# VectorE's instruction order and the 16x16 inverse in the chunk pipeline of a bidirectional encoder layer

## The chip, the cores and the metric

One NeuronCore of a Trainium2 chip runs the whole program. The metric is the device time of one execution in microseconds; a measurement is the median of several executions. Engines: PE (TensorE), DVE (VectorE), ACT (ScalarE), POOL (GpSimd) and SP (SyncE, which here issues all DMAs).

## The reference

Two layers of an encoder are applied to 2,560 tokens (a sequence of 2,048 and one of 512). Layer 0 holds two gated linear recurrences. Layer 1 holds a banded attention (8 heads, window 128) and an RWKV-7 time mixing (8 heads of 64, both directions). The change touches layer 1 alone. The part of it that the kernel has to compute in chunks is the scan

```
def step(S, inp):
    r_t, w_t, k_t, v_t, kk_t, b_t = inp
    s_kk = jnp.einsum('bhvk,bhk->bhv', S, kk_t)
    S = S * w_t[:, :, None, :] - s_kk[..., None] * b_t[:, :, None, :] + v_t[..., None] * k_t[:, :, None, :]
    return S, jnp.einsum('bhvk,bhk->bhv', S, r_t)
```

In chunks of 64 tokens this needs, for each chunk and head, the inverse of a 64x64 unit triangular matrix, some Gram products, and a short sequential chain over chunks. The attention beside it is

```
s = jnp.einsum('bnigrd,bnjgd->bngrij', qb, kb).astype(jnp.float32) * (hd ** -0.5)
lse = jnp.logaddexp(jax.nn.logsumexp(s, axis=-1), sink_b)
p = jnp.exp(s - lse[..., None])
```

## The kernel before

The program runs layer 0, then layer 1's projections, then `layer1_core` (the stage of this change), then the output projection. `layer1_core` has 20 steps (4 head pairs by 5 blocks of 512 tokens; each step holds both directions, 16 chunk-heads of 128 rows). Its work is written as generators ("lanes"), each `yield` ending one round's share, and a loop over rounds takes one share of every lane in the order C, T, A, X:

- A (`stageA`, 10 rounds a step, five for each half): Gram products `gramb`, `gramk`, then `bk`, `kt`, `av`; DVE multiplies them with masks into `GB`, ACT copies, POOL sorts the 32x32 diagonal blocks into `LD` and `OF`. In the sixth round (second half) it also builds `LC` from the 16x16 blocks (`L1` on POOL, `LC` on DVE) and stores it to DRAM (`lm`). `load` prefetches the next half's `Z`, `KR`, `vs` by DMA, four buffers deep.
- `inverse` (called whole at the end of every tenth round, round 8 of each step): reads `lm` back as `A`, so that each of 128 partitions holds one 16x16 block; inverts it on DVE by back substitution, 14 times a product into `tp` and an add into `A` (L1370, L1372); stores it to DRAM (`tm`), reads it back as `TC`, and spreads it into `TE` and, transposed, `TT` (L1378, L1380).
- T (`stageT`, 10 rounds, starting at round 12 with the first step): with `TE` and `TT` it doubles the blocks to 32 and 64 rows (`px`, `py`, DVE and ACT evacuate), then for each half `t1` (ACT copies it), `finx` (DVE adds it into `RX`) and `fino` (ACT copies it into `OH`).
- C (`chain`, 8 rounds of each 10, starting at round 20): 16 small matmuls `chain`, then one DVE add that makes the next state `S0` (named S in the trace); every fourth time DVE also adds the outputs into `od`, which go to DRAM.
- X (`attention`, 40 units of five rounds): scores of two heads, scores of two more with the normalisation on DVE (`nm`, `se`, `den`, `rd`, four scalings of `pr`, with ACT's exponentials between), `po` and DVE's `yo`, and two rounds of transposes `pt`.

A scheduler orders each engine's queue from a simulated timeline, program order deciding among what is ready there. PE alone is exempt: inside this stage `pin` ties each matmul to the one before it, so PE's queue follows the source order. The queues of DVE, ACT, POOL and SP are the scheduler's. Every engine takes its own queue strictly in order, so an instruction that waits holds all behind it.

PSUM tiles: `pg` and `pT` (lanes A and T) hold one buffer each, `pa` (attention: `score`, `pt`, `po`) two, so PE can often start a lane's next product only when DVE or ACT has read the one before.

Of the kernel before, what the change touches and what calls it, by code (L numbers as in the profile page):

```python
# [10 lines left out]
F32 = mybir.dt.float32  # L11
# [4 lines left out]
ALU = mybir.AluOpType  # L16
# [22 lines left out]


class Common:
    def __init__(self, ctx, tc, a, seqs):
        self.ctx, self.tc, self.nc, self.a = ctx, tc, tc.nc, a
        self.seqs = seqs
        self.T = sum(n for _, n in seqs)
        self.nblk = self.T // NB
        self.blk_seq = []
        for s, (o, n) in enumerate(seqs):
            self.blk_seq += [s] * (n // NB)
        nc = self.nc  # L50
        self.const = ctx.enter_context(tc.tile_pool(name="const", bufs=1))
        self.dram = ctx.enter_context(tc.tile_pool(name="dram", bufs=1, space=DRAM))
        self.lanes = {}
        self.pt_tag = "t"
        self.pinned = []
        nc.scalar.preload_act_table_set("natural_log_exp_and_others")
        self.eps6 = self.cst("eps6", 1e-6)
        self.eps5 = self.cst("eps5", 1e-5)
        self.ident = self.load_const("ident", [128, 128])
        self.ones = self.const.tile([128, 128], F32R, name="onesm")  # L60
        self.act(self.ones, self.ident, AF.Copy, bias=1.0 / 128.0, scale=0.0)
# [53 lines left out]
    def tt(self, out, a, b, op, eng=None):  # L115
        (eng or self.nc.vector).tensor_tensor(out=out, in0=a, in1=b, op=op)  # L116

    def stt(self, out, a, s, b, op0, op1, eng=None):
        (eng or self.nc.vector).scalar_tensor_tensor(out=out, in0=a, scalar=s, in1=b, op0=op0, op1=op1)  # L119

    def ts(self, out, a, s1, s2, op0, op1=None, eng=None):
        eng = eng or self.nc.vector
        if op1 is None:
            eng.tensor_scalar(out=out, in0=a, scalar1=s1, scalar2=None, op0=op0)
        else:
            eng.tensor_scalar(out=out, in0=a, scalar1=s1, scalar2=s2, op0=op0, op1=op1)

    def mm(self, out, lhsT, rhs, start=True, stop=True):
        self.pin(self.nc.tensor.matmul(out=out, lhsT=lhsT, rhs=rhs, start=start, stop=stop))  # L129

    def pin(self, ins):

        if self.pinned:
            if len(self.pinned) > 1:
                self.tc.add_manual_dep(ins.ins, self.pinned[1], mybir.DependencyInfo(
                    mybir.DependencyClass.NoSync, mybir.DependencyReason.DATA), reason="order")
            self.pinned = [True, ins.ins.name]

# [11 lines left out]
    def tr(self, out, in_):  # L150
        n = in_.shape[0]
        self.pin(self.nc.tensor.transpose(out, in_, self.ident[0:n, 0:n]))  # L152

# [693 lines left out]
class Odd(Even):  # L847
# [369 lines left out]
    def layer1_core(self):  # L1217
        tc, nc, a = self.tc, self.nc, self.a
        with ExitStack() as ctx:
# [46 lines left out]

            loaded = []

# [21 lines left out]
            def stageA(n):  # L1290
# [4 lines left out]
                LO = lp.tile([128, 16, 32], F32, tag="LO", bufs=2, name="LO")  # L1295
                data[n] = (OF, LO)
                for hf in range(2):
                    cs = slice(4 * hf, 4 * hf + 4)
# [12 lines left out]
                    for hd in range(2):  # L1311
                        for i, blk in enumerate((B1[hd], B2[hd])):
                            nc.gpsimd.tensor_copy(b4(LD)[blk, :, cs], gs[blk, :, :, 32 * i:32 * i + 32])
                    if hf == 1:

                        LC = lp.tile([128, 16, 16], F32, tag="LC", bufs=1, name="LC")
                        L1 = lp.tile([128, 16, 16], F32, tag="L1", bufs=1, name="L1")
                        self.tt(L1, LD[:, :, 16:32], M1, ALU.mult, nc.gpsimd)
                        self.tt(LC, LD[:, :, 0:16], M0, ALU.mult)
                        self.tt(LC, LC, L1, ALU.add)  # L1320
                        nc.sync.dma_start(out=lms[n % 2].rearrange("d c p t -> p (d c) t"), in_=LC)
                        nc.gpsimd.memset(LO[:, :, 0:16], 0.0)
                        self.tt(LO[:, :, 16:32], LD[:, :, 16:32], MO, ALU.mult, nc.gpsimd)
                    for hd in range(2):
# [37 lines left out]
            def inverse(n):  # L1362

                A = self.wk.tile([128, 16, 16], F32, tag="A", bufs=2, name="A")
                nc.sync.dma_start(out=A, in_=lms[n % 2].rearrange("d c (g s) t -> (d c g) s t", s=16))
                tp = self.wk.tile([128, 64], F32, tag="tp", bufs=1, name="tp")
                for j in range(14, 0, -1):
                    w = 15 - j
                    t3 = tp[:, 0:j * w].rearrange("p (a b) -> p a b", b=w)
                    self.tt(t3, A[:, 0:j, j:j + 1].to_broadcast([128, j, w]),  # L1370
                            A[:, j:j + 1, j + 1:16].to_broadcast([128, j, w]), ALU.mult)
                    self.tt(A[:, 0:j, j + 1:16], A[:, 0:j, j + 1:16], t3, ALU.add)  # L1372
                nc.vector.memset(A[:].rearrange("p a b -> p (a b)")[:, 0:256:17], 1.0)
                nc.sync.dma_start(out=tms[n % 2].rearrange("d c (g s) t -> (d c g) s t", s=16), in_=A)
                TC = lp.tile([128, 16, 16], F32, tag="TC", bufs=1, name="TC")
                nc.sync.dma_start(out=TC, in_=tms[n % 2].rearrange("d c p t -> p (d c) t"))
                te, tt = small("TE"), small("TT")
                self.tt(te.rearrange("p c (a t) -> p c a t", t=16),  # L1378
                        TC.unsqueeze(2).to_broadcast([128, 16, 2, 16]), ME, ALU.mult)
                nc.vector.transpose(out=tt, in_=te)  # L1380
                tes.append(te)
                tts.append(tt)

            def stageT(n):
# [17 lines left out]
                self.tt(te, te, y, ALU.add)  # L1402
                nc.vector.transpose(out=tt, in_=te)
                for i in range(2):
# [9 lines left out]
                nc.scalar.copy(xs[B2[0]], x[B2[0]])  # L1414
                nc.vector.tensor_copy(xs[B2[1]], x[B2[1]])
                yield
# [4 lines left out]
                nc.scalar.copy(TL[B1[0], :, 32:64], y[B1[0]])  # L1421
                nc.vector.tensor_copy(TL[B1[1], :, 32:64], y[B1[1]])
                yield
# [40 lines left out]
            def chain(n):  # L1464
# [7 lines left out]
                for hf in range(2):  # L1472
# [3 lines left out]
                    for c in range(4):  # L1476
                        if S0[0] is None:
                            S0[0] = OH[:, :, 0, 64:128]
                            for d in range(2):
                                nc.vector.tensor_copy(o4[d][:, 0], OH[:, d, 0, 0:64])  # L1480
                            i = 1
                        else:
                            z = S0[0]
                            for d in range(2):
                                for q in Q:
                                    self.mm(po[q, d, 4 + c], RX[q, d, c, 64:128], z[q, d])
                            for d in range(2):
                                for q in Q:
                                    self.mm(po[q, d, c], z[q, d], RX[q, d, c, 0:64])
                            s0 = self.wk.tile([128, 2, 64], F32, tag="S0", bufs=3, name="S0")  # L1490
                            self.tt(s0, po[:, :, 4 + c], OH[:, :, c, 64:128], ALU.add)
                            S0[0] = s0
# [19 lines left out]
            self.ln_exp()  # L1512
            self.pinned = [True]
            lanes = dict(C=seq(chain), T=seq(stageT), A=seq(stageA), X=self.attention())
            start = dict(A=0, X=0, T=12, C=20)
            for r in range(5 * (2 * N + 6)):
                for x in ("C", "T", "A", "X"):
                    if r < start[x] or x == "C" and (r - start[x]) % 5 == 4:
                        continue
                    next(lanes[x], None)  # L1520
                if r >= 8 and (r - 8) % 10 == 0 and (r - 8) // 10 < N:
                    inverse((r - 8) // 10)
                self.tick()
            assert all(next(g, "end") == "end" for g in lanes.values())
            self.pinned = []
            self.drain()
# [82 lines left out]
    def attend(self, g, b, qt, s0, s1, keys, msk, snk, nsk):  # L1609
# [17 lines left out]
        for hd in range(4):  # L1627
            ps = self.pa.tile([128, 384], F32, tag="s", name="score")
            for i in range(2):
                self.mm(ps[:, 0:nk], q[:, hd], K[:, i, k0 - w0:k1 - w0], start=(i == 0), stop=(i == 1))  # L1630
            pr = ap.tile([128, 384], F32, tag="ptmp", bufs=5, name="pr")
            h = 4 * g + hd
            nc.vector.tensor_tensor_reduce(pr[:, 0:nk], ps[:, 0:nk], msk[:, m0:m0 + nk], -0.125,  # L1633
                                           nsk[:, h:h + 1], ALU.add, ALU.min, nm[:, hd:hd + 1])
# [9 lines left out]
        rd = ap.tile([128, 4], F32, tag="rd", name="rd")  # L1644
        nc.vector.reciprocal(out=rd, in_=den)
        for hd in range(4):
# [134 lines left out]
```

## Time and profile before

| what | us |
|---|---|
| median of 3 runs (lowest, highest) | 4200.91 (4189.49, 4204.29) |
| the profiled execution, device time | 4210.02 |
| its span from first to last instruction | 4208.2 |
| PE busy over the span | 3572.8 (85%) |
| DVE busy | 2432.1 (58%) |
| ACT busy | 1900.4 (45%) |
| POOL busy | 844.1 (20%) |
| mean granted TensorE clock, share of full | 0.916 |

The profiled execution's own time is 2 us above its span and 9 us above the median of the three runs. Layer 1's core takes the span from about 2,640 to 3,870 us; its steady part repeats with one step of 10 rounds. Busy shares are averages over four stages with different limits, so the stage has to be read by itself.

### The profile page before, as it was taken

The page shows a single profiled execution, that of the slowest core. Times are in us where ns is not written, and L with a number is a line of the kernel's source. Part 1 is how long each engine was busy: PE and PEld are TensorE (multiplying, and loading weights), DVE is VectorE, ACT ScalarE, POOL GpSimd, SP SyncE. Part 2 cuts the span into 40 slices and gives each one's busy share as a digit, 9 for nine tenths or more (in the row PEclk, how much of TensorE's full clock was granted, in tenths as well). Part 3 has the DMA queues.
Part 4 walks back from the last instruction along what each step waited for, and adds up shares of the span by engine and source line. Part 5 has one row for each costly group of instructions (what it writes and reads, how often), then busy time and mean ns, then how long its engine had stood idle before and what let it go on. Part 6 is the DMA issues. An engine that isn't in the chain of part 4 may idle for free.

```text
span 4208.2 us, 95158 instructions
## 1 busy us (share of the span) xinstructions
PE 3572.8 (85%) x39928; PEld 2865.3 (68%) x39928; DVE 2432.1 (58%) x4888; ACT 1900.4 (45%) x3394; POOL 844.1 (20%) x1013
## 2 busy tenths in 40 slices
PE   6999999998888699998999898687777777776689
PEld 4878787776776578776777676466556666655477
DVE  4554545457666678466574757445445455444687
ACT  4565657455455532355463446333333333333450
POOL 1020212112222232224132322222112111211000
PEclk8999999999899799999999999788888888887799
DMA  7544544456545488677677775533333333333685
GB/s 274 200 153 153 187 149 175 167 183 235 221 180 204 136 261 268 221 248 237 239 269 229 238 260 203 145 89 99 106 94 92 100 100 84 96 99 99 200 294 186
DMA packets 646285, 754.43 MB, mean 179 GB/s; under 512 B 188352, under 2 KB 512576, under 8 KB 620256
## 3 DMA queue, kind: packets, MB, share of 16 engines
q1 hardware_dynamic: 645856, 748.34, 54.2%
q8 instruction: 314, 5.14, 0.5%
q14 instruction: 115, 0.94, 0.1%
HBM read 518.51 MB, written 220.20 MB: 176 GB/s over the span
## 4 chain that ended last, share of the span: by engine, by line
PE 27%; DMA 9%; DVE 7%; issue 5%; ACT 2%; POOL 2%; SPq 1%; DVEq 0%; POOLq 0%; ACTq 0%
PE pp L129 13%; DMA lm<-LC 2%; PE po L129 1%; PE chain L129 1%; DVE tp L116 1%; DMA h<-h_scr 1%; PE py L129 1%; PE px L129 1%; DVE A L116 1%; PE pt L152 1%; DMA A<-lm 1%; PE fino L129 1%; PE gramb L129 1%; DMA tm<-A 1%; PE score L129 1%
## 5 line engine op out<-in xcount | busy, mean ns | idle before, releaser
L129 PE MATMUL pp<-h,whi 128*128 128x512 f32 (+2 forms) x4800 | 1570.4, 406 | 100.0 <-DMA h<-h_scr 42.1
L129 PEld LDWEIGHTS pp<-h,whi 128*128 128x128 f32 (+2 forms) x4800 | 896.6, 191 | 316.0 <-DMA h<-h_scr 45.0
L129 PE MATMUL pp<-h,wlo 128*128 128x512 f32 (+2 forms) x2400 | 960.2, 401 | 6.1 <-POOL wlo L116 6.0
L129 PEld LDWEIGHTS pp<-h,wlo 128*128 128x128 f32 (+2 forms) x2400 | 456.7, 190 | 114.7 <-POOL wlo L116 9.2
L113 ACT ACT_TABLE_LOAD x227 | 291.2, 1283 | 22.9 <-DVE cl L506 12.4
L129 PE MATMUL pp<-owh,oh 128*128 128x512 f32 x640 | 255.9, 400 | 21.7 <-DMA oh<-o_scr 21.7
L129 PE MATMUL pp<-owh,ol 128*128 128x512 f32 x640 | 251.4, 394 | 4.9 <-DMA ol<-o_scr 4.9
L129 PE MATMUL pp<-owl,oh 128*128 128x512 f32 x640 | 253.6, 396 | 0.0
L116 POOL TENSOR_TENSOR wlo<-wst,whi 128x512 fp32r<-128x512 f32 (+3 forms) x87 | 158.3, 1826 | 278.4 <-ACT whi L113 267.5
L1635 ACT ACTIVATE pr<-pr,nm 128x384 f32<-128x384 f32 (+1 forms) x160 | 93.8, 587 | 240.7 <-DVE nm L1633 217.0
L116 POOL TENSOR_TENSOR tmp<-tmp 128x512 fp32r<-128x512 f32 x80 | 120.7, 1509 | 238.5 <-ACT tmp L113 175.9
L116 POOL TENSOR_TENSOR at<-abuf,abuf 64x256 f32<-64x256 f32 x80 | 63.9, 799 | 517.8 <-DVE abuf L536 448.2
L152 PE MATMUL pt<-c_ident,pr 128*128 128x128 f32 x448 | 77.3, 303 | 102.9 <-DVE yo L116 91.9
L129 PEld LDWEIGHTS pp<-owh,oh 128*128 128x128 f32 x640 | 122.7, 192 | 49.6 <-DMA oh<-o_scr 24.5
L129 PEld LDWEIGHTS pp<-owh,ol 128*128 128x128 f32 x640 | 121.5, 190 | 32.4 <-DMA ol<-o_scr 6.8
L1633 DVE CUSTOM_DVE_ANT_0 pr<-score,amask,nsink 128x384 f32<-128x384 f32 (+1 forms) x160 | 88.3, 585 | 90.6 <-PE score L129 90.5
L129 PEld LDWEIGHTS pp<-owl,oh 128*128 128x128 f32 x640 | 122.9, 192 | 25.1
L113 ACT ACTIVATE tmp<-tmp 128x512 fp32r<-128x512 f32 (+2 forms) x165 | 103.7, 629 | 67.5 <-DVE tmp L119 50.8
L152 PEld LDWEIGHTS pt<-c_ident,pr 128*128 128x128 f32 x448 | 51.6, 151 | 118.5 <-issue 103.0
L129 PE MATMUL po<-pT,vw 128*128 128x512 f32 x224 | 122.8, 687 | 5.2 <-DVE nm L1633 4.7
L129 PE MATMUL score<-kw,q 128*128 128x384 f32 (+1 forms) x320 | 86.6, 398 | 42.2 <-DVE nm L1633 30.5
L116 DVE TENSOR_TENSOR tp<-A 128x14 f32<-128x14 f32 (+6 forms) x280 | 65.2, 233 | 95.9 <-DMA A<-lm 87.8
(325 smaller groups left out, 7301.8 us busy)
## 6 DMA issues: line engine op xcount, KB each, us to landing
h<-h_scr SPq DMA_DIRECT2D x70, 2048.0 KB, 9.1
h<-h_scr SPq DMA_DIRECT2D x80, 1024.0 KB, 7.4
z_scr<-Z SPq DMA_DIRECT2D x40, 1024.0 KB, 5.0
h_scr<-h SPq DMA_DIRECT2D x10, 2048.0 KB, 7.4
oh<-o_scr SPq DMA_DIRECT2D x40, 512.0 KB, 5.0
ol<-o_scr SPq DMA_DIRECT2D x40, 512.0 KB, 6.4
h_scr<-h1s SPq DMA_DIRECT2D x20, 1024.0 KB, 4.9
Zc<-z_scr SPq DMA_DIRECT2D x80, 256.0 KB, 3.5
```

The lines of the kernel that those rows point to most:

```text
L113: self.nc.scalar.activation(out=out, in_=in_, func=func, bias=bias, scale=scale)
L116: (eng or self.nc.vector).tensor_tensor(out=out, in0=a, in1=b, op=op)
L129: self.pin(self.nc.tensor.matmul(out=out, lhsT=lhsT, rhs=rhs, start=start, stop=stop))
L152: self.pin(self.nc.tensor.transpose(out, in_, self.ident[0:n, 0:n]))
L1633: nc.vector.tensor_tensor_reduce(pr[:, 0:nk], ps[:, 0:nk], msk[:, m0:m0 + nk], -0.125, nsk[:, h:h + 1], ALU.add, ALU.min, nm[:, hd:hd + 1])
L1635: nc.scalar.activation(out=pr[:, 0:nk], in_=pr[:, 0:nk], func=AF.Exp, bias=nm[:, hd:hd + 1], scale=-1.0, accum_out=den[:, hd:hd + 1])
```

## The change

A small class `InOrder` wraps an engine: each instruction issued through it gets an ordering dependency (without a semaphore) on the one before it. Inside the round loop both `self.pe` and `self.vec` are such wrappers, and the helpers `tt`, `stt`, `ts` and the direct DVE calls of this stage go through `self.vec`; so DVE's queue now follows the source order as PE's did. (`pin` is gone; PE's order is made by the same class.)

`inverse` becomes a lane, I, last in each round and starting at round 6, with yields that spread it over 10 rounds. Counting rounds of a step from A's first, 0 to 9: round 6 builds `LC` and issues the store and the read-back; rounds 8 and 9 do five back-substitution columns each; round 0 of the next step does the last four, stores and reads back; round 2 makes `TE` and `TT`; T's first round is now round 3. `L1` moves from POOL to DVE; `LC`, `L1` and `LO` move from lane A into lane I. T and C start one round later (13 and 21 for 12 and 20).

```
+class InOrder:
+    def __init__(self, tc, eng):
+        self.tc, self.eng, self.prev = tc, eng, None
+
+    def __getattr__(self, name):
+        def call(*args, **kwargs):
+            ins = getattr(self.eng, name)(*args, **kwargs)
+            if self.prev is not None:
+                self.tc.add_manual_dep(ins.ins, self.prev, mybir.DependencyInfo(
+                    mybir.DependencyClass.NoSync, mybir.DependencyReason.DATA), reason="order")
+            self.prev = ins.ins.name
+            return ins
+        return call
...
     def tt(self, out, a, b, op, eng=None):
-        (eng or self.nc.vector).tensor_tensor(out=out, in0=a, in1=b, op=op)
+        (eng or self.vec).tensor_tensor(out=out, in0=a, in1=b, op=op)
...
     def mm(self, out, lhsT, rhs, start=True, stop=True):
-        self.pin(self.nc.tensor.matmul(out=out, lhsT=lhsT, rhs=rhs, start=start, stop=stop))
+        self.pe.matmul(out=out, lhsT=lhsT, rhs=rhs, start=start, stop=stop)
...
@@ stageA @@
-                    if hf == 1:
-
-                        LC = lp.tile([128, 16, 16], F32, tag="LC", bufs=1, name="LC")
-                        L1 = lp.tile([128, 16, 16], F32, tag="L1", bufs=1, name="L1")
-                        self.tt(L1, LD[:, :, 16:32], M1, ALU.mult, nc.gpsimd)
-                        self.tt(LC, LD[:, :, 0:16], M0, ALU.mult)
-                        self.tt(LC, LC, L1, ALU.add)
-                        nc.sync.dma_start(out=lms[n % 2].rearrange("d c p t -> p (d c) t"), in_=LC)
-                        nc.gpsimd.memset(LO[:, :, 0:16], 0.0)
-                        self.tt(LO[:, :, 16:32], LD[:, :, 16:32], MO, ALU.mult, nc.gpsimd)
@@ inverse @@
+                LD, LO = diag.pop(n)
+
+                LC = lp.tile([128, 16, 16], F32, tag="LC", bufs=1, name="LC")
+                L1 = lp.tile([128, 16, 16], F32, tag="L1", bufs=1, name="L1")
+                self.tt(L1, LD[:, :, 16:32], M1, ALU.mult)
+                self.tt(LC, LD[:, :, 0:16], M0, ALU.mult)
+                self.tt(LC, LC, L1, ALU.add)
+                nc.sync.dma_start(out=lms[n % 2].rearrange("d c p t -> p (d c) t"), in_=LC)
+                nc.gpsimd.memset(LO[:, :, 0:16], 0.0)
+                self.tt(LO[:, :, 16:32], LD[:, :, 16:32], MO, ALU.mult, nc.gpsimd)
                 A = self.wk.tile([128, 16, 16], F32, tag="A", bufs=2, name="A")
                 nc.sync.dma_start(out=A, in_=lms[n % 2].rearrange("d c (g s) t -> (d c g) s t", s=16))
+                yield
+                yield
                 tp = self.wk.tile([128, 64], F32, tag="tp", bufs=1, name="tp")
                 for j in range(14, 0, -1):
...
                     self.tt(A[:, 0:j, j + 1:16], A[:, 0:j, j + 1:16], t3, ALU.add)
-                nc.vector.memset(A[:].rearrange("p a b -> p (a b)")[:, 0:256:17], 1.0)
+                    if j in (10, 5):
+                        yield
+                self.vec.memset(A[:].rearrange("p a b -> p (a b)")[:, 0:256:17], 1.0)
                 nc.sync.dma_start(out=tms[n % 2].rearrange("d c (g s) t -> (d c g) s t", s=16), in_=A)
                 TC = lp.tile([128, 16, 16], F32, tag="TC", bufs=1, name="TC")
                 nc.sync.dma_start(out=TC, in_=tms[n % 2].rearrange("d c p t -> p (d c) t"))
+                yield
+                yield
                 te, tt = small("TE"), small("TT")
...
-                nc.vector.transpose(out=tt, in_=te)
+                self.vec.transpose(out=tt, in_=te)
                 tes.append(te)
                 tts.append(tt)
+                for _ in range(4):
+                    yield
...
@@ the round loop @@
-            self.pinned = [True]
-            lanes = dict(C=seq(chain), T=seq(stageT), A=seq(stageA), X=self.attention())
-            start = dict(A=0, X=0, T=12, C=20)
+            self.pe, self.vec = InOrder(tc, nc.tensor), InOrder(tc, nc.vector)
+            lanes = dict(C=seq(chain), T=seq(stageT), A=seq(stageA), X=self.attention(), I=seq(inverse))
+            start = dict(A=0, X=0, I=6, T=13, C=21)
             for r in range(5 * (2 * N + 6)):
-                for x in ("C", "T", "A", "X"):
-                    if r < start[x] or x == "C" and (r - start[x]) % 5 == 4:
-                        continue
-                    next(lanes[x], None)
-                if r >= 8 and (r - 8) % 10 == 0 and (r - 8) // 10 < N:
-                    inverse((r - 8) // 10)
+                for x in ("C", "T", "A", "X", "I"):
+                    if r >= start[x] and not (x == "C" and (r - start[x]) % 5 == 4):
+                        next(lanes[x], None)
                 self.tick()
```

## Rows read from the trace of the kernel before

**Rows 1.** Engine busy over 19 whole steps of the stage (span, engines, clock, DMA).
```profile
2681.90:3815.60 1133.70, 858.55 (x24792) 702.56 (x24792) 556.73 (x1678) 398.81 (x884) 211.28 (x389) 0.86 0.35 94
```

**Rows 2.** The transpose that ends the inverse, by its source line.
```profile
L1380 DVE STREAM_TRANSPOSE TT<-TE x20: 711/711/714, 2681.9 to 3815.6; 128x512 f32<-128x512 f32 x20
```

**Rows 3.** Who waited for whom, 2660 to 3800 us: total, times, longest.
```profile
PE pt L152 <- DVE yo L116: 90.7, 19, 11.0
...
DVE tp L116 <- DMA A<-lm: 87.8, 20, 5.7
...
DVE TE L116 <- DMA TC<-tm: 77.9, 19, 6.1
...
PE fino L129 <- DVE RX L116: 36.6, 13, 6.1
...
PE score L129 <- DVE nm L1633: 27.1, 7, 5.2
...
PE px L129 <- issue: 19.5, 16, 2.5
...
PE kt L129 <- issue: 17.5, 8, 3.2
...
PE bk L129 <- issue: 17.1, 9, 2.2
...
PE score L129 <- DVE A L1373: 10.8, 3, 3.7
```

**Rows 4.** Timeline of DVE within one step: start, duration, instruction, idle before.
```profile
3010.14 0.42 DVE L116 TENSOR_TENSOR LC<-LC,L 128x256 f32<-128x256 f32 x1
...
3016.30 0.17 DVE L116 TENSOR_TENSOR tp<-A 128x14 f32<-128x14 f32 x1 [3.54 <-DMA A<-lm]
...
3027.71 0.17 DVE L116 TENSOR_TENSOR A<-A,tp 128x14 f32<-128x14 f32 x1
3027.80 0.85 DVE L116 TENSOR_TENSOR yo<-po,gt 64x256 f32<-64x256 f32 x2
3032.96 0.69 DVE L116 TENSOR_TENSOR TE<-TC,mkb 128x512 f32<-128x512 f32 x1 [4.30 <-DMA TC<-tm]
3033.68 0.71 DVE L1380 STREAM_TRANSPOSE TT<-TE 128x512 f32<-128x512 f32 x1
3034.43 1.23 DVE L116 TENSOR_TENSOR RX<-finx,KR 128x1024 f32<-128x1024 f32 x1
...
3047.87 0.62 DVE L1633 CUSTOM_DVE_ANT_0 pr<-score,amask,nsink 128x384 f32<-128x384 f32 x1
...
3050.07 1.41 DVE L124 TENSOR_SCALAR pr<-pr,rd 128x384 f32<-128x384 f32 x4
```

**Rows 5.** Timeline of PE around the same step.
```profile
3002.50 1.10 PE L129 MATMUL gramb<-KR,Zc 64*64 64x128 f32 x32
...
3004.34 0.45 PE L129 MATMUL chain<-S,RX 64*64 64x64 f32 x8
...
3028.80 0.87 PE L152 MATMUL pt<-c_ident,pr 128*128 128x128 f32 x3 [5.96 <-DVE yo L116]
...
3031.87 1.93 PE L129 MATMUL gramb<-KR,Zc 64*64 64x128 f32 x32
```

**Rows 6.** Instruction groups, 2660 to 3800 us: count, busy us, mean ns, idle before.
```profile
L116 DVE TENSOR_TENSOR tp<-A 128x14 f32<-128x14 f32 (+6 forms) x267 | 62.5, 234 | 95.5 <-DMA A<-lm 87.8
...
L116 POOL TENSOR_TENSOR LO<-LD,mkb 128x256 f32<-128x256 f32 x20 | 14.6, 731 | 0.0
L116 DVE TENSOR_TENSOR LC<-LC,L 128x256 f32<-128x256 f32 x20 | 14.6, 729 | 18.5 <-POOL L L116 18.5
...
L116 DVE TENSOR_TENSOR LC<-LD,mkb 128x256 f32<-128x256 f32 x19 | 8.1, 425 | 13.9 <-POOL LD L1313 13.9
```

**Rows 7.** The prefetch of KR: one issue in SP's timeline.
```profile
3035.68 0.91 SPq L1283 DMA_DIRECT2D KR<-z_scr  x2
```

**Rows 8.** DMA issues, 2660 to 3800 us: count, KB each, median us to landing.
```profile
KR<-z_scr SPq DMA_DIRECT2D x72, 256.0 KB, 3.2
```

More of the change, by code (lines that the diff above doesn't have):

```diff
@@ L54, in __init__ @@
         self.pt_tag = "t"
-        self.pinned = []
+        self.pe, self.vec = nc.tensor, nc.vector
         nc.scalar.preload_act_table_set("natural_log_exp_and_others")
@@ L115, in tt @@
     def tt(self, out, a, b, op, eng=None):
-        (eng or self.nc.vector).tensor_tensor(out=out, in0=a, in1=b, op=op)
+        (eng or self.vec).tensor_tensor(out=out, in0=a, in1=b, op=op)
     def stt(self, out, a, s, b, op0, op1, eng=None):
-        (eng or self.nc.vector).scalar_tensor_tensor(out=out, in0=a, scalar=s, in1=b, op0=op0, op1=op1)
+        (eng or self.vec).scalar_tensor_tensor(out=out, in0=a, scalar=s, in1=b, op0=op0, op1=op1)
     def ts(self, out, a, s1, s2, op0, op1=None, eng=None):
-        eng = eng or self.nc.vector
+        eng = eng or self.vec
         if op1 is None:
@@ L128, in mm @@
     def mm(self, out, lhsT, rhs, start=True, stop=True):
-        self.pin(self.nc.tensor.matmul(out=out, lhsT=lhsT, rhs=rhs, start=start, stop=stop))
[L131 to L137, printed above, removed]
+        self.pe.matmul(out=out, lhsT=lhsT, rhs=rhs, start=start, stop=stop)
     def split(self, x, hi, lo, eng=None):
@@ L151, in tr @@
         n = in_.shape[0]
-        self.pin(self.nc.tensor.transpose(out, in_, self.ident[0:n, 0:n]))
+        self.pe.transpose(out, in_, self.ident[0:n, 0:n])
     def ln_exp(self):
@@ L1265, in layer1_core @@
             tms = [self.dram.tile([2, 8, 128, 16], F32, name=f"tm{i}") for i in range(2)]
-            loaded = []
+            loaded, diag = [], {}
             def load(u):
@@ L1296, in stageA @@
                 data[n] = (OF, LO)
+                diag[n] = (LD, LO)
                 for hf in range(2):
@@ L1402, in stageT @@
                 self.tt(te, te, y, ALU.add)
-                nc.vector.transpose(out=tt, in_=te)
+                self.vec.transpose(out=tt, in_=te)
                 for i in range(2):
@@ L1414, in stageT @@
                 nc.scalar.copy(xs[B2[0]], x[B2[0]])
-                nc.vector.tensor_copy(xs[B2[1]], x[B2[1]])
+                self.vec.tensor_copy(xs[B2[1]], x[B2[1]])
                 yield
@@ L1421, in stageT @@
                 nc.scalar.copy(TL[B1[0], :, 32:64], y[B1[0]])
-                nc.vector.tensor_copy(TL[B1[1], :, 32:64], y[B1[1]])
+                self.vec.tensor_copy(TL[B1[1], :, 32:64], y[B1[1]])
                 yield
@@ L1479, in chain @@
                             for d in range(2):
-                                nc.vector.tensor_copy(o4[d][:, 0], OH[:, d, 0, 0:64])
+                                self.vec.tensor_copy(o4[d][:, 0], OH[:, d, 0, 0:64])
                             i = 1
@@ L1512, in layer1_core @@
             self.ln_exp()
-            self.pinned = [True]
-            lanes = dict(C=seq(chain), T=seq(stageT), A=seq(stageA), X=self.attention())
-            start = dict(A=0, X=0, T=12, C=20)
+            self.pe, self.vec = InOrder(tc, nc.tensor), InOrder(tc, nc.vector)
+            lanes = dict(C=seq(chain), T=seq(stageT), A=seq(stageA), X=self.attention(), I=seq(inverse))
+            start = dict(A=0, X=0, I=6, T=13, C=21)
             for r in range(5 * (2 * N + 6)):
-                for x in ("C", "T", "A", "X"):
-                    if r < start[x] or x == "C" and (r - start[x]) % 5 == 4:
-                        continue
-                    next(lanes[x], None)
-                if r >= 8 and (r - 8) % 10 == 0 and (r - 8) // 10 < N:
-                    inverse((r - 8) // 10)
+                for x in ("C", "T", "A", "X", "I"):
+                    if r >= start[x] and not (x == "C" and (r - start[x]) % 5 == 4):
+                        next(lanes[x], None)
                 self.tick()
             assert all(next(g, "end") == "end" for g in lanes.values())
-            self.pinned = []
+            self.pe, self.vec = nc.tensor, nc.vector
             self.drain()
@@ L1632, in attend @@
             h = 4 * g + hd
-            nc.vector.tensor_tensor_reduce(pr[:, 0:nk], ps[:, 0:nk], msk[:, m0:m0 + nk], -0.125,
+            self.vec.tensor_tensor_reduce(pr[:, 0:nk], ps[:, 0:nk], msk[:, m0:m0 + nk], -0.125,
                                            nsk[:, h:h + 1], ALU.add, ALU.min, nm[:, hd:hd + 1])
@@ L1644, in attend @@
         rd = ap.tile([128, 4], F32, tag="rd", name="rd")
-        nc.vector.reciprocal(out=rd, in_=den)
+        self.vec.reciprocal(out=rd, in_=den)
         for hd in range(4):
```

## The prediction

> **What bounds the kernel now.** I read the busy time of the stage first, then the waits, then one step in the timelines of DVE and PE. The change leaves the other stages alone, so its worth is read from `layer1_core`. From the first to the twentieth transpose that ends an inverse the trace has 19 equal steps [rows 2]: (3815.6 - 2681.9)/19 = 59.67 us each. In that stretch PE is busy 858.55 us, 45.2 a step, and so idle 14.5 us a step; DVE is busy 556.73/19 = 29.3 us a step, ACT 21.0, POOL 11.1 [rows 1]. No engine is full. Since PE's queue is in source order and every lane passes through it, the stage is as long as PE's work plus PE's waits.
>
> The list of waits says what those are [rows 3]; it covers 1140 us, 19.1 steps. PE waited 90.7 us at `pt` for DVE's `yo`, 36.6 at `fino` for `RX`, 27.1 and 10.8 at `score` for DVE: 165.2 us, 8.65 a step. Another 19.5 + 17.5 + 17.1 = 54.1 us, 2.83 a step, are waits of PE at `px`, `kt` and `bk` that are put to "issue": PE waited for nothing that the profile shows. And DVE itself, idle half of the time, waited 87.8 us for `A` and 77.9 for `TC`, the two trips of the inverse through DRAM: 8.7 a step, as much as PE lost to DVE.
>
> The timeline shows how one becomes the other [rows 4, 5]. DVE adds up `LC` until 3010.56; the first use of `A` starts at 3016.30, after 3.54 us of idle DVE. The back substitution ends at 3027.88 and only then does `yo` run, although `po` had been ready long before: it stands behind the inverse in DVE's queue. PE's transposes share their two buffers with `po`, so they sat idle 5.96 us until 3028.80. Then `TE`, next in DVE's queue, waits 4.30 us for `TC`, and `RX`, which needs nothing of the inverse, runs behind it at 3034.43; `fino` needs `RX`. The scheduler placed the inverse as if its DMAs came back sooner than they do.
>
> [...] The same 32 `gramb` matmuls took 1.10 us before this wait and 1.93 us 3 us after it [rows 5].
>
> **The change, part by part.** All positions are rounds 0 to 9 of a step; a round is 4.5 us of PE work on average (45.2/10).
>
> Waits for the two trips. `LC` is now done at the end of round 6 and `A` first used at the end of round 8; the last column is done in round 0 and `TE` made at the end of round 2. Each trip has some two rounds, 9 us. The first took 3016.30 - 3010.56 = 5.7 us, the second 3032.96 - 3027.88 = 5.1 [rows 4]. Both are hidden behind PE's work of those rounds, and removed is what they cost PE: 8.65 us a step. If the cover failed, each would again hold DVE for what lies beyond it, and now with everything behind it (a rival below).
>
> A new wait in its place. `TE` and `TT` are the last DVE work of round 2, behind that round's normalisation, and `px`, right behind the 16 chain matmuls of round 3, needs `TT`. The normalisation cannot start before PE's last work of the round, the scores. From the start of the last `pr` to the end of the scalings DVE took 3051.48 - 3047.87 = 3.61 us (ACT's exponentials lie inside), and `TE` to the end of `TT` 1.43 [rows 4]: 5.04. PE has only the chain in that time, 0.45 us for half of its overlapping matmuls [rows 5], 0.6 together by my estimate. PE waits 4.4 us a step. Bounds: 5.0 with no cover; half, if DVE gets ahead because PE is slower than I think. I take 4.4. Behind `px`, `kt` and `po` wait with it; DVE's S0 adds stand behind `TT` too, but the next chain is needed one round later.
>
> Order in the other rounds. DVE's heaviest place is round 7 into 8: the normalisation ends 3.6 us after the scores, then S0 and `RX` (1.23) follow, `RX` ready about 5.1 after the scores, while PE has round 8 and the chain of round 9 before `fino`, 4.5 to 5: a wait of 0.4, taken. In round 6 DVE does `pr`, then `LC`; in rounds 8, 9 and 0 some ten instructions of the inverse each at 0.234 us [rows 6], about 2.3 us, after everything that PE needs in the next round. I cost these at nothing: DVE's 29.3 us against PE's 45.2 leave 1.6 us a round, and the inverse is last in its round. If that cover were gone, the 28 instructions would cost up to 28 x 0.234 = 6.6 us a step.
>
> `L1` on DVE. The same operation as the `LC` product, 0.425 us [rows 6], at the end of round 6; PE needs DVE's next result (S0) a round later, so nothing. Without the cover 20 x 0.43 = 9 us. The row shows more: the `LC` add, of the same size, has a mean of 0.729, while POOL runs `LO` (0.731) on the same `LD`. By that difference `L1` costs 0.43 + 0.30, and 15 us in all if uncovered. [...]
>
> DMAs. The number is unchanged, but T starts a round later, and with it the buffer of `KR` comes free later: the load for round 0 waits for `RX` of round 8 instead of round 7. `RX` at 5.1 after round 7's scores, plus 0.91 to issue both [rows 7] and 3.2 to land [rows 8], is 9.2; `gramb` comes after two rounds of PE work and the `t1` of round 0, over 9.0. I cost it at nothing; uncovered by 3 us, it would cost 60 in all. On SP's queue the store and read-back of `LC` pass the loads of rounds 6 to 8; no cost beyond the rivals.
>
> Clock. [...] The waits of rows 3 number 42 on DVE and 33 on issue, 3.9 a step; after the change 1 and 1.7. [...]
>
> Issue waits. `px`, `kt` and `bk` lie in rounds 2 to 4, where PE now waits for `TT` anyhow. I let the overlap save half, 1.4; bounds 0 and 2.8.
>
> Last, T and C start one round later: one more round in a run of 230, at most 6.0 us (59.67/10); I take 5.
>
> Sum: 8.65 - 4.4 - 0.4 + 2.0 + 1.4 = 7.25 us a step, 145 over 20 steps, less 5: 140. The profiled execution took 4210, so 4070; it stood 9 above the median of the runs, so 4061.
>
> **The rivals.**
> [...]
> *Less:* `KR` arrives late by 3 us in each step and holds `gramb`: 4.25 a step, 80 in all, 4121. Without the clock and issue terms too, 0.85 a step, 4189. For it: the margin above is thin. Against: SP has had `RX`-released loads out at once [rows 7].
> *No change:* each wait on DVE is replaced by one of the same length, because PE, not DVE, is what limits. For it: PE is busy 45.2 of 59.67 us and DVE 29.3. The time stays at 4201. Against: the waits of rows 3 end at DVE work that stood behind a DMA. [...]
> *Slower:* the read-back of `A` stands on SP behind a `vs` load that waits for `fino` of round 9. [...] It decides from 7 us of new holds a step. Against: it needs both trips nearly doubled.
>
> **How the numbers follow.** Forecast 0.58 (own range 4000 to 4110), more 0.13, less 0.14, no change 0.06, slower 0.09. I call 0.5%, 21 us, what can be told from no change: faster 0.85, same 0.06, slower 0.09. The range 3970 to 4190 leaves out some 0.07 below and 0.12 above.
>
> **What would show it.** The transposes of L1380 should stand 52 us apart. DVE's waits for `A` and `TC` should nearly vanish, PE's for `yo`, `RX` and `score` fall below 30 us together, and a new row, PE `px` for DVE `TT`, should have some 85 us in 20 waits. The granted clock of the stage should rise above 0.88. Waits of `gramb` for `KR` would show the rival "less"; DVE waits for `A` or `TC` of several us each, the rival "slower". The forecast is wrong if a DVE instruction in source order waits on a partner (ACT's exponential, a DMA) with PE's next need behind it, in a round where I saw slack.

## The result and the profile after

The changed kernel takes 4068.67 us (median of 4 runs, 4062.51 to 4082.42) against 4201.84: a ratio of 0.9693, 95% interval 0.9659 to 0.9727. The prediction was 4061. The profiled execution took 4082.42 us, 127.6 less than that of before. Of this 125.6 lie in `layer1_core`, between its first `gramb` and its last `od` (2639.0 to 3876.9 us before, 2636.2 to 3748.5 after).

In the new kernel most operations of the stage carry the wrapper's line, L49, so they are told apart by tile. First the stretch from the first `TE` to the nineteenth, 18 steps, in the view of rows 1 (span; PE, PEld, DVE, ACT, POOL busy; clock; DMA):

```profile
2681.67:3647.34 965.67, 791.85 (x23748) 644.85 (x23748) 555.50 (x1618) 383.45 (x846) 189.01 (x360) 0.89 0.40 108
```

A step takes 965.67/18 = 53.65 us, of which PE is busy 44.0. The clock is 0.89, up from 0.86 [rows 1]. Over all 19 intervals, from the `TE` at 2681.67 to the one at 3693.21, a step is 53.24 us against 59.67 [rows 2]: 6.43 us less, times 20 is 129.

Now the waits, those that answer to rows 3 (2660 to 3680 us, 19 steps; total, times, longest):

```profile
PE px L49 <- DVE TT L49: 84.3, 19, 5.1
...
PE px L49 <- issue: 22.5, 17, 2.6
...
PE av L49 <- issue: 17.2, 6, 3.7
...
PE fino L49 <- DVE RX L49: 14.2, 21, 1.3
...
PE gramb L49 <- issue: 9.5, 9, 2.8
...
PE bk L49 <- issue: 8.8, 7, 1.8
...
PE gramb L49 <- DMA KR<-z_scr: 5.0, 9, 1.3
...
PE kt L49 <- issue: 3.1, 3, 1.2
...
DVE tp L49 <- DMA A<-lm: 0.5, 1, 0.5
```

The rows of PE at `pt` for `yo` and at `score` for `nm` and for `A` are gone, and so is DVE's wait for `TC` in this stretch; DVE's wait for `A` fell from 87.8 us to 0.5. What took their place is above all one wait, `px` for `TT`, 4.44 us a step. The timeline of DVE shows why it stands where it does:

```profile
3000.01 0.16 DVE L49 TENSOR_TENSOR den<-den,se 128x4 f32<-128x4 f32 x1 [0.73 <-ACT se L130]
3000.20 0.18 DVE L49 RECIPROCAL rd<-den 128x4 f32<-128x4 f32 x1
3000.42 1.41 DVE L49 TENSOR_SCALAR pr<-pr,rd 128x384 f32<-128x384 f32 x4
3001.74 0.69 DVE L49 TENSOR_TENSOR TE<-TC,mkb 128x512 f32<-128x512 f32 x1
3002.46 0.71 DVE L49 STREAM_TRANSPOSE TT<-TE 128x512 f32<-128x512 f32 x1
3003.10 0.25 DVE L49 TENSOR_TENSOR S<-chain,OH 128x128 f32<-128x128 f32 x1
3013.15 0.86 DVE L49 TENSOR_TENSOR yo<-po,gt 64x256 f32<-64x256 f32 x2 [9.80 <-PE po L49]
```

`TE` and `TT` run without a pause behind the normalisation. After one more `S` add DVE has nothing to do for 9.80 us, until PE, which was held up before `px`, has run `px`, `kt` and `po`. PE's own timeline of these microseconds:

```profile
3003.32 1.50 PE L49 MATMUL px<-TT,LO 32*32 32x32 f32 x95 [4.49 <-DVE TT L49]
3006.65 0.69 PE L49 MATMUL px<-TT,LO 32*32 32x32 f32 x33 [1.83 <-issue]
3007.26 1.13 PE L49 MATMUL kt<-II,KR 64*64 64x64 f32 x32
3008.32 4.72 PE L49 MATMUL po<-pT,vw 128*128 128x512 f32 x6
```

After 4.49 us for `TT`, 95 of the 128 `px` matmuls run, and then PE stops again for 1.83 us with nothing to wait for that the profile shows. That second wait turned out to be the most telling of the study. What comes behind the wait is slower too: from 3003.32 to 3007.34 us the granted clock is 0.50, the lower of the two levels, 0.50 and 1.00, that the record of this execution holds, and over `po` it is 0.60. These six `po` matmuls take 4.72 us; six of the same take 2.84 at 3029.84 us, where the clock is 1.00. At each of the 19 waits for `TT` the clock falls to 0.50, 0.4 to 4.9 us after the wait's start: during the wait, or up to 0.75 us behind it.

### The profile page after: what moved, and what is told of

Read it like the earlier page. It is cut to its first block, busy times and chain, and to the rows that moved or that the text cites. A ratio compares the mean times of both kernels' runs of the same rounds, so it can differ in the third digit from the quotient of the medians.

```text
span 4080.6 us, 95107 instructions
## 1 busy us (share of the span) xinstructions
PE 3535.0 (87%) x39928; PEld 2832.2 (69%) x39928; DVE 2453.8 (60%) x4908; ACT 1901.9 (47%) x3394; POOL 825.3 (20%) x993
## 5 line engine op out<-in xcount | busy, mean ns | idle before, releaser
L49 PE MATMUL po<-pT,vw 128*128 128x512 f32 x224 | 133.7, 741 | 0.0
L49 PE MATMUL px<-TT,LO 32*32 32x32 f32 x2560 | 40.2, 234 | 105.8 <-DVE TT L49 84.3
L49 DVE TENSOR_TENSOR yo<-po,gt 64x256 f32<-64x256 f32 x80 | 33.6, 420 | 163.0 <-PE po L49 147.0
L49 DVE CUSTOM_DVE_ANT_0 pr<-score,amask,nsink 128x384 f32<-128x384 f32 (+1 forms) x160 | 87.7, 585 | 58.9 <-PE score L49 58.9
L133 POOL TENSOR_TENSOR tmp<-tmp,yh 128x512 fp32r<-128x512 f32 x40 | 56.3, 1409 | 316.0 <-ACT yh L130 227.0
L49 PEld LDWEIGHTS px<-TT,LO 32*32 32x32 f32 x2560 | 36.9, 147 | 109.3 <-issue 109.1
```

The costliest lines, as they stand in the source:

```text
L49: ins = getattr(self.eng, name)(*args, **kwargs)
L133: (eng or self.vec).tensor_tensor(out=out, in0=a, in1=b, op=op)
```

## The experiments

All times are medians, all ratios against the kernel before. The table's columns are microseconds a step, over 18 steps from the first to the nineteenth `TE`: the step, PE busy (view by windows), and the sum of all PE rows in the list of waits by what ended them. Worked out in this way, before is 59.84 us a step.

| kernel | us | ratio (95%) | step | PE busy | waits on DVE | on issue | on ACT, DMA, PE |
|---|---|---|---|---|---|---|---|
| before | 4201.8 | | 59.84 | 45.2 | 9.85 | 4.09 | 0.74 |
| after | 4068.7 | 0.9693 (0.9659 to 0.9727) | 53.65 | 44.0 | 5.49 | 3.82 | 0.39 |
| order_only | 4137.9 | 0.9857 (0.9828 to 0.9885) | 56.32 | 43.5 | 9.50 | 3.56 | 0 |
| spread_only | 4211.5 | 1.0024 (1.0008 to 1.0040) | 60.67 | 47.0 | 9.37 | 3.92 | 0.36 |
| i_before_x | 4033.0 | 0.9601 (0.9573 to 0.9629) | 50.98 | 42.7 | 2.21 | 5.51 | 0.55 |
| te_early | 4007.5 | 0.9541 (0.9515 to 0.9567) | 50.26 | 43.4 | 2.01 | 4.51 | 0.41 |
| te_front | 4024.4 | 0.9584 (0.9567 to 0.9601) | 50.72 | 43.1 | 1.48 | 5.73 | 0.29 |
| l1_pool | 4067.8 | 0.9684 (0.9647 to 0.9721) | 53.55 | 43.8 | 5.51 | 3.82 | 0.50 |
| columns_whole | 4069.0 | 0.9678 (0.9653 to 0.9703) | 53.51 | 44.1 | 5.01 | 4.02 | 0.37 |
| kr5 | 4064.1 | 0.9676 (0.9656 to 0.9696) | 53.42 | 43.9 | 5.72 | 3.73 | 0.14 |
| wide_px | 3921.0 | 0.9333 (0.9317 to 0.9348) | 45.95 | 40.8 | 1.40 | 2.87 | 0.83 |
| whole_early | 4004.0 | 0.9531 (0.9511 to 0.9551) | 49.88 | 43.0 | 1.70 | 4.99 | 0.29 |

**The two halves of the change, each alone.** order_only keeps the old inverse (whole, at the end of round 8, with `LC` in lane A and the old starts), but issues it through `self.vec`:

```
             self.pe, self.vec = InOrder(tc, nc.tensor), InOrder(tc, nc.vector)
-            lanes = dict(..., X=self.attention(), I=seq(inverse))
+            lanes = dict(..., X=self.attention())
...
+                if r >= 8 and (r - 8) % 10 == 0 and (r - 8) // 10 < N:
+                    inverse((r - 8) // 10)
```

> VectorE in source order, but the inverse whole at the end of round 8 as before (LC in lane A, L1 on POOL, T and C at rounds 12 and 20). Theory 1, the order is what gains, because it takes PE's next needs out from behind the trips: A's trip (5.7 us) is over by round 8, since LC is done in round 5, so DVE is held in one piece only, 28 x 0.234 = 6.6 us of columns, 5.1 for TC and 1.4 for TE and TT, 13 us; PE has rounds 9 and 0 (some 8 us) before it needs a DVE result from behind, so it waits 5 to 7 us a step: 4070 to 4150, and one long wait of PE a step on S, RX or GB instead of the 4.4 us at px. Theory 2, the spreading is what gains, because in-order DVE with the whole inverse in one place holds everything for 13 us: no gain, 4180 to 4260, waits of over 9 us a step.

It took 4137.9 us, inside the range of theory 1. PE does have one long wait in every step, but of 6.4 to 11.9 us where 5 to 7 were expected, and PE's waits on DVE sum to the 9.5 us a step that theory 2 spoke of. The long wait stands at `fino` for `RX` in 7 of the 18 steps, at `gramk` for `GB` in one and at `chain` for `S` in the others. DVE's and PE's timelines of a step of the first kind:

```profile
3012.55 0.69 DVE L49 TENSOR_TENSOR TE<-TC,mkb 128x512 f32<-128x512 f32 x1 [4.46 <-DMA TC<-tm]
3013.27 0.71 DVE L49 STREAM_TRANSPOSE TT<-TE 128x512 f32<-128x512 f32 x1
```

```profile
3015.47 0.49 PE L49 MATMUL fino<-GB,T 64*64 64x64 f32 x8 [9.58 <-DVE RX L49]
```

DVE stands 4.46 us before `TE` with `RX` behind it, and PE stands 9.58 us before `fino`. So order alone leaves the sum of PE's waits on DVE where it was (9.50 against 9.85) and still gains 1.4%: PE is busy 1.7 us less for the same matmuls, and the waits on ACT, 0.74, are gone. There are also fewer interruptions: 2.1 waits on DVE a step against 3.0. That fewer and longer waits cost less of the clock fits this (the mean clock of the profiled execution is 0.923, against 0.916 before), but was not isolated; and the count alone does not decide it, since i_before_x below has 3.6 waits on DVE a step and PE is busy less still (42.7).

spread_only is the changed kernel with DVE's queue left to the scheduler:

```
-            self.pe, self.vec = InOrder(tc, nc.tensor), InOrder(tc, nc.vector)
+            self.pe, self.vec = InOrder(tc, nc.tensor), nc.vector
```

> The inverse as a lane over ten rounds, T and C a round later, L1 on VectorE, but VectorE's queue left to the scheduler (PE alone in source order). Theory 1 (order gains): the scheduler still places the columns and TE where its simulated DMA has landed, so DVE waits for A and TC stay at several us a step, with yo, RX and pr behind them: 4130 to 4200. Theory 2 (spreading gains): with the inverse later in program order other work goes first, the DVE waits for A and TC nearly vanish, 4050 to 4090.

No gain at all, 4211.5, some 10 above before and above even theory 1's range of 4130 to 4200. Theory 2 falls: the trips are back in DVE's queue, 61.1 and 62.6 us in 16 waits each, and PE waits behind them (2660 to 3640 us):

```profile
DVE TE L133 <- DMA TC<-tm: 62.6, 16, 4.5
DVE tp L133 <- DMA A<-lm: 61.1, 16, 5.0
...
PE po L49 <- DVE nm L1648: 52.6, 17, 6.5
...
PE score L49 <- DVE nm L1648: 39.6, 15, 3.9
PE fino L49 <- DVE RX L133: 38.4, 15, 3.0
```

The two yields around each trip only change the program order; a queue that is not bound to it does not keep them. So the whole gain needs both: 64 us less from order alone, some 10 more from spreading alone, 133 less from the two together.

**The new wait.** Three kernels move `TE` and `TT` away from behind the normalisation. i_before_x puts lane I ahead of lane X in every round:

```
-                for x in ("C", "T", "A", "X", "I"):
+                for x in ("C", "T", "A", "I", "X"):
```

> As after, with lane I ahead of lane X in each round, so that TE and TT of round 2 stand ahead of the normalisation. My account of the new wait (84 us of PE at px behind the normalisation): that wait falls below 15 us, TE waits some 1 to 2 us for TC instead, which PE does not feel, and the time falls by 70 to 110 us to 3960 to 4000. Rival: the columns and LC, now ahead of pr and yo in rounds 6, 8, 9 and 0, make PE wait at score and pt by as much: 4050 to 4090, with waits of score or pt on DVE of over 40 us.

te_early takes `TE` one round sooner:

```
                 nc.sync.dma_start(out=TC, in_=tms[n % 2].rearrange("d c p t -> p (d c) t"))
                 yield
-                yield
...
-                for _ in range(4):
+                for _ in range(5):
                     yield
```

> As after, with TE and TT at the end of round 1 instead of round 2 (one round between the store of A and TE instead of two). My account: DVE then waits 1 to 2 us a step for TC at the end of round 1, with S and pr of round 2 behind, PE's wait at px for TT falls below 15 us, and the time is 3960 to 4010. Rival, that the second round of cover for the trip of TC is needed: DVE waits for TC over 3 us a step and PE waits for S or pr instead of TT: 4050 to 4090.

te_front changes the order of lanes in round 2 alone:

```
+                for x in (("C", "T", "A", "I", "X") if r % 10 == 2 else ("C", "T", "A", "X", "I")):
```

> As after, but in round 2 alone lane I goes ahead of lane X, so TE and TT stand ahead of the normalisation and nothing else of lane I moves. My account: PE's wait at px for TT falls from 84 us to below 15, DVE waits less than 1 us a step for TC (two rounds of cover remain, less the normalisation), nothing else is held: 3985 to 4015, at or below the kernel with TE at the end of round 1 (4007). Rival, that PE's instruction waits fill whatever is freed: waits of PE on issue rise from 3.8 to over 6 us a step and the time stays at 4030 to 4070.

In all three the wait for `TT` nearly vanishes and the time falls, by 36, 61 and 44 us against after. The account of the wait holds; its price does not. In te_front waits on DVE fall by 4.0 us a step, but the step only by 2.9, and waits on issue rise from 3.82 to 5.73, 41.7 us of them at `px` itself (2660 to 3600 us):

```profile
PE px L49 <- issue: 41.7, 24, 4.4
...
PE kt L49 <- issue: 13.2, 4, 3.8
...
PE px L49 <- DVE TT L49: 7.5, 8, 1.9
```

The wait for `TT` had covered a part of a wait on issue. So both i_before_x and te_front came out between my account and the rival (4033 where 3960 to 4000 was expected, 4024 where 3985 to 4015). te_early came out inside its range (3960 to 4010), near the upper end, and a part of its rival is in its trace: DVE waits 36.2 us in 19 waits for `TC`, and PE 20.7 us in 23 waits at `chain` for the `S` that stands behind it (2660 to 3600 us). Why te_early, which waits more for DVE than te_front, has fewer waits on issue (4.51 against 5.73) stays open.

**What "issue" is.** wide_px is te_front with `px` and `py` of rounds 3 to 6 issued for every second chunk-head with 64 columns:

```
-                for c in range(16):
+                for c in range(0, 16, 2):
                     for g in range(4):
                         q = slice(32 * g, 32 * g + 32)
-                        self.mm(x[q, c], LO[q, c], tt[q, c])
+                        self.mm(x[q, c:c + 2].rearrange("p a t -> p (a t)"), LO[q, c],
+                                tt[q, c:c + 2].rearrange("p a t -> p (a t)"))
```

and the like for the other three products.

> As te_front (4024 us, 5.7 us a step of PE waits put to issue), but px and py of stage T (rounds 3 to 6) are issued for every second chunk-head only, each with 64 columns instead of 32: the same columns in half the instructions, 384 fewer matmuls and weight loads a step of some 2600. It leaves out half of these products (the neighbouring chunk-head gets the wrong left factor). Theory, that issue is PE's instruction supply, which bursts of small matmuls outrun: the issue waits at px and those behind fall with the count, to under 3.5 us a step, and the time by 40 us or more to 3950 to 3985. Rival, that issue has nothing to do with the number of instructions: the issue waits stay above 5 us a step and the time falls only by what px and py themselves take less, some 1 us a step, to 3995 to 4025.

It took 3921.0 us, 103 less than te_front and 29 below even the theory's range. Waits on issue halved, 5.73 to 2.87. The groups of te_front over its 18 steps and, below, of wide_px (2674 to 3500 us, 18 steps but for the first 12 `px` matmuls) show count, busy us, mean ns of one, and the idle time before them: half as many matmuls, each a little longer.

```profile
L49 PE MATMUL py<-TE,XS 32*32 32x32 f32 x3456 | 45.8, 193 | 4.9 <-issue 4.9
L49 PE MATMUL px<-TT,LO 32*32 32x32 f32 x2304 | 28.8, 200 | 42.4 <-issue 34.8 <-DVE TT L49 7.5
L49 PE MATMUL px<-TT,OF 32*32 32x32 f32 x1152 | 23.5, 193 | 6.1 <-issue 5.9
```

```profile
L49 PE MATMUL py<-TE,XS 32*32 32x64 f32 x1728 | 40.0, 218 | 0.3 <-issue 0.2
L49 PE MATMUL px<-TT,LO 32*32 32x64 f32 x1140 | 23.2, 227 | 14.4 <-issue 10.5 <-DVE TT L49 3.8
L49 PE MATMUL px<-TT,OF 32*32 32x64 f32 x576 | 19.6, 215 | 0.5 <-DVE TT L49 0.3
```

Per step that is 98.1/18 = 5.45 us busy against 82.8/18 = 4.60: 0.85 less, of a step that is 4.8 shorter. The waits on issue carry 2.9, and PE's other work takes 1.4 less at a clock that rose from 0.93 to 0.97; PE's waits on ACT and DMAs rose by 0.5. The queue that the page calls instruction, in the page of te_front and of wide_px (packets, MB):

```profile
q8 instruction: 314, 5.14, 0.5%
```

```profile
q8 instruction: 284, 4.65, 0.5%
```

The program has 7,679 instructions fewer (95,100 to 87,421) and 30 packets fewer: 256 instructions, 16.4 KB, a packet. These are PE's: its 80,456 records in te_front, sequencer's included, and its 72,776 in wide_px make 314 and 284 packets of 256. So issue waits halved where PE's instructions became fewer. 128 small matmuls with their weight loads are as many instructions as a packet holds, and `py` runs 128 in 1.29 us (at 3013.59 us in after). That such bursts run ahead of PE's instruction supply is my reading of these counts; how long one packet takes to come was not measured.

**Three costs taken as nothing.** l1_pool puts `L1` back (`ALU.mult, nc.gpsimd`).

> As after, with L1 back on POOL. The prediction costed L1 on VectorE at nothing, because it stands at the end of round 6 with PE's next need a round later: within 0.3% of 4069. Rival, that it is not covered: 9 to 15 us less, 4054 to 4060. The LC add should again stand against POOL's operation on the same tile and rise from 0.425 to some 0.73 us.

4067.8: no difference. The interval of the medians, some 16 us either way, could not tell the rival's 9 to 15 us by itself; the step of the trace can, 53.55 us against 53.65, 2 us in 20 steps. The second half of the expectation was wrong, the `LC` add stayed at 0.425 us (below). columns_whole removes the `yield` inside the column loop and adds two behind the store:

```
-                    if j in (10, 5):
-                        yield
...
+                yield
+                yield
```

> As after, with all 14 columns in round 8 in one piece, and TE still in round 2, so that both trips have two rounds or more. Theory A, that the trips are what had to be spread: DVE is 4.5 us later at the end of round 8, but S of round 9 is not needed before round 1, so PE hardly feels it: 4060 to 4090. Theory B, that the 28 instructions in one piece hold DVE too long, up to 6.6 us a step as the prediction bounded it: 4130 to 4200, with waits of PE on S, GB or fino of over 3 us a step.

4069.0, theory A: spreading the columns is worth nothing that can be told (a step is 53.51 us), so what spreading adds comes with the trips. kr5 gives `KR` and `vs` `bufs=NS + 1`.

> As after, with five buffers of KR and vs instead of four, so that their loads no longer wait for RX and fino of the step before. In after PE waits 0.35 us a step for these and neighbouring DMAs at gramb; the prediction costed that at nothing. If the margin is that thin and no thinner: these waits go, 5 to 10 us less, 4058 to 4066. Rival, that KR late hides more behind other waits: 25 us less or more.

4064.1, within the noise of 4068.7; the DMA waits fell from 0.35 us a step to 0.09. The margin was as thin as computed, and what it let through is small.

**The favoured parts together.** whole_early has all columns in round 8, `TE` at the end of round 1 and five buffers.

> The parts that the runs favour together: all columns in round 8, TE and TT at the end of round 1 with three rounds for TC's trip, five buffers of KR and vs. DVE should wait for neither trip and PE for no TT; what is left is issue at 4 to 5.5 us a step and RX at 0.8. If the TC wait at the end of round 1 is what te_early (4007) still paid: 3985 to 4003. If freed time is filled by issue waits: 4003 to 4025.

4004.0, the fastest of those that leave nothing out, not distinguishable from te_early, and at the border of the two ranges, so the time does not choose between them. The waits do in part: those on DVE fell by 0.3 us a step against te_early, those on issue rose by 0.5, to 4.99.

## Why the prediction was right, and where its terms were off

Time, sign and mechanism were right: two trips taken out of DVE's queue, one new wait at `px`. By terms, in us a step:

- *Waits removed and added.* Predicted 8.65 less, 4.4 and 0.4 more, net 3.85. Measured on all rows 9.85 to 5.49, net 4.36. The wait for `TT` was 84.3/19 = 4.44, `fino` for `RX` 14.2/19 = 0.75. The 3.61 + 1.43 us of [rows 4], less the chain, were the right sum.
- *The clock.* The 2.0 less in the sum is my estimate, and no run shows it; what the runs show in its place is PE's busy time, which fell by 1.2 at a clock that rose from 0.86 to 0.89. The number of PE's waits was to fall from 3.9 a step to 2.7. The number of waits on DVE and on issue, on all rows, fell only from 6.1 to 5.6 a step, and the new wait brings the lower level with it, as `po` above shows; the prediction counted it as one wait like any other.
- *Issue waits*, the term that failed. Predicted 1.4 less because the wait for `TT` overlaps them; measured 0.27 less. The rows that the step named did fall, from 54.1 us [rows 3] to 22.5 + 8.8 + 3.1 (`kt`), 1.0 a step; but new ones came at `av` (17.2) and `gramb` (9.5). They go by the count of instructions and not by the round (5.73 to 2.87 in wide_px, and 31 of 33 at one place of each 256 in the last section); that less waiting on DVE brings more of them fits the rise from 3.82 to 5.73 in te_front.
- *Not in the sum.* PE's waits on ACT, 0.74 in before, ended; waits on DMAs at `gramb`, costed at nothing, took 0.35, and 0.04 was PE's own.

The terms measured add up to 4.36 + 1.2 + 0.27 + 0.35 = 6.2 us against 7.25 predicted, 21 us short over 20 steps (16 by the 6.43 of all 19 intervals). That the time was met within 8 us is in part luck: the extra round, taken at 5 us, cost about 3 (129 us by steps, 125.6 by the stage), 2 us were saved outside the stage, and the profiled execution of after stands 14 us above the median of its runs where that of before stood 8. By the profiled executions alone the gain is 127.6 us where 140 was predicted.

Of the rivals, "less" by way of `KR` was right in place and wrong in size (0.35 us a step, and 5 us in all by kr5, within the noise). "More" did not come, since the wait at `px` was 4.44 us a step where 4.4 had been taken; nor did "slower", since DVE waited 0.5 us in all for `A` and for `TC` not at all in the 19 steps. "No change", PE as the limit, was wrong for this change, but its reason returned one step later: of the 4.0 us a step of waits on DVE that went, 1.9 came back as waits of PE on issue (te_front). The 133 us lay in waits of the busiest engine, PE (45.2 of 59.67 us), and what ended them was an engine at half load, DVE (29.3), whose order was wrong.

## What to carry to other kernels

Here the DMA round trips in DVE's queue (8.7 us a step of its waits) cost what stood behind them (8.65 us a step of PE's waits): put a trip's far end where nothing that another engine needs soon follows, and bind the queue to that order; here order alone gave half of the gain and spreading alone none. A wait that goes may uncover another at the same place, as at `px`, where the waits for `TT` fell from 84.3 us (after) to 7.5 (te_front) and those on issue rose from 22.5 to 41.7; the price of a wait is what the next one leaves of it. A wait of PE also cost behind its end here, where the clock had fallen (six `po` matmuls in 4.72 us at 0.60, in 2.84 at 1.00): compare the same matmuls at both levels. Before chasing the last waits of a PE that runs thousands of tiny matmuls, count instructions: wide_px, with half as many of them at `px` and `py`, took 103 us less than te_front.

## What the runs showed of the hardware

*Order in a queue.* In before DVE stood 5.75 us at `TE` for `TC`, until 2729.09, with two `od` copies behind it whose `OH` ACT had finished at 2722.39; they ran at 2730.45. POOL stood 7.59 us at `KR` for DVE's `RX`, until 3647.93, with the copies of `LD` behind it, whose `GS` was there from 3644.84; they ran at 3648.92. ACT stood 5.95 us at `se` for DVE's `se`, until 3501.28, with the copy of `kt` behind it, whose matmuls had ended at 3496.95; it ran at 3502.28.

*Instruction supply.* PE waits with no releaser, the longest 3.7 us in after, are 3.6 to 5.7 us a step in every version with all its instructions, and 2.87 in wide_px, which has fewer. Counted through PE's records (matmuls, weight loads and the sequencer's) in order of start, 31 of the 33 issue waits over 0.9 us of after (2660 to 3680 us) stand at one and the same place in each 256, to within one record, and so do 33 of 33 in before (2660 to 3800 us) and 24 of 24 in wide_px; this is a count, not a view. 256 is also the number of instructions in a packet, by the 7,679 instructions and 30 packets of wide_px. Not every such place shows a wait: it is 31 of 196 in this stretch of after. But these 31 sum to 56.5 us, of 71.2 us of issue waits in all, 3.8 us in a step of 53.65.

*VectorE beside GpSimd.* The mean of 0.729 us of the `LC` add [rows 6], which the prediction took as one price, is a mix of two durations: 8 of the 20 adds took 0.41 to 0.42 us [rows 4], and 12, all begun 0.07 to 0.08 us after POOL's `LO`, took 0.94. One of the longer ones, on DVE and on POOL:

```profile
2705.03 0.94 DVE L116 TENSOR_TENSOR LC<-LC,L 128x256 f32<-128x256 f32 x1 [1.55 <-POOL L L116]
```

```profile
2704.96 0.73 POOL L116 TENSOR_TENSOR LO<-LD,mkb 128x256 f32<-128x256 f32 x1
```

It began 0.07 us after `LO` and ended 0.28 after it, and took 0.94 where the other eight took 0.42; whether it stood still for most of `LO` or ran more slowly, no view shows. In the changed kernel the `LC` operations no longer meet POOL, and all 20 adds took 0.42 to 0.43 us. But more of the columns do: in before 24 of the 533 products and adds of the columns overlapped an operation of POOL and took 0.60 us in the mean, the other 509 took 0.20 (2660 to 3800 us); in after 152 of 536 overlapped one and took 0.40, the other 384 took 0.20 (2660 to 3680 us). Beside POOL's copies of `LD`, and of `OF` right behind them, five in a row took 0.37 to 0.40 us; operations of these sizes (128x44, 128x36, 128x26) have means of 0.18 to 0.20 in before. The mean of the products rose from 0.234 [rows 6] to 0.279, other POOL operations than these copies included:

```profile
3042.98 0.37 DVE L49 TENSOR_TENSOR tp<-A 128x44 f32<-128x44 f32 x1
3043.38 0.40 DVE L49 TENSOR_TENSOR A<-A,tp 128x44 f32<-128x44 f32 x1
3043.82 0.40 DVE L49 TENSOR_TENSOR tp<-A 128x36 f32<-128x36 f32 x1
3044.25 0.40 DVE L49 TENSOR_TENSOR A<-A,tp 128x36 f32<-128x36 f32 x1
3044.69 0.39 DVE L49 TENSOR_TENSOR tp<-A 128x26 f32<-128x26 f32 x1
```

```profile
3042.47 1.70 POOL L1323 COPY LD<-GS 32x256 f32<-32x256 f32 x4 [7.58 <-ACT GS L1319]
3044.21 0.83 POOL L1325 COPY OF<-GS 32x256 f32<-32x256 f32 x2
```

```profile
L49 DVE TENSOR_TENSOR tp<-A 128x14 f32<-128x14 f32 (+6 forms) x268 | 74.8, 279 | 8.4 <-DMA A<-lm 0.5
```
